# Mixture-of-experts stage of a two-block kernel: transposes moved into the products, full-height index matmuls, contiguous weight units

## The chip, the cores and the metric

The kernel runs on one core of a Trainium2 chip. Time is the device time of one execution in microseconds (us), as the median of several runs; lower is better. The profile is one further execution, recorded by the hardware profiler.

## The reference

The reference is two transformer-like blocks over 1024 tokens of 1024 channels, all in float32. The first block has a modulated RMS norm, an mLSTM and a Fourier branch, and then a mixture of experts in which each of 16 experts chooses its 128 tokens. The second block is a mixer of five branches with an output projection. The change touches the expert stage most, which is this:

```python
def expert_choice(h, w_router, w_gate, w_up, w_down):
    cap = CAP_FACTOR * l // N_EXPERTS                     # 128 tokens for each expert
    aff = jax.nn.softmax(jnp.einsum('bld,de->ble', h, w_router).astype(jnp.float32), axis=-1)
    vals, idx = lax.top_k(jnp.swapaxes(aff, 1, 2), cap)
    xs = h[bidx, idx]
    hid = jax.nn.silu(jnp.einsum('becd,edf->becf', xs, w_gate)) * jnp.einsum('becd,edf->becf', xs, w_up)
    y = jnp.einsum('becf,efd->becd', hid, w_down) * vals[..., None].astype(h.dtype)
    return jnp.zeros_like(h).at[bidx, idx].add(y)
```

Each of the three matrices of an expert is 1024 x 1024 float32, 4 MB.

## The kernel before

**Exact products.** Every float32 operand of a large product is split into a float32r part `hi` and a remainder `lo`; `mm3` (line 354) adds three matmuls, hi*hi, hi*lo and lo*hi. A matmul here has 128 rows, 128 stationary columns and 512 moving columns.

**Weights.** All weights pass through one list of units of 1 MB, 8 KB for each of the 128 partitions, made in `add_px` (line 577). `_issue` loads the next unit on SyncE's (SP's) DMA queue, in the order of the list, into a slot named `raw`. `_split` (line 234) makes slots named `w` from it: ScalarE writes `hi`, VectorE writes `lo`. A unit of an expert matrix holds two blocks of 128 rows and gives two `w` slots, each good for six matmuls. There are 25 slots of 8 KB a partition in all; `prefetch` (line 263) keeps up to 6 split `w` slots live, 5 ahead of the product, and gives the slots that are left to raw units. `pick` takes the free slot whose last user is due to finish first. An expert matrix unit is read by `k2` (line 605) as two pieces of 4 KB for each partition, 512 KB apart in DRAM.

**Experts.** `experts` (line 1629) works on one expert after the other. `index(e)` (line 1657) finds the tokens of expert e: two matmuls whose operands have 48 rows, each followed by a VectorE count over 512 columns, and a small add. `gather(e)` fetches the 128 token rows by an indirect DMA on GpSimd's (POOL's) queue into `xs`. `transp` (line 1676) turns a 128 x 1024 tile with eight TensorE transposes in two groups of four; after each group ScalarE writes 512 columns of `hi` and VectorE 512 columns of `lo` of a slot named `xT`. `prod` (line 1690) is one product: eight steps k of six matmuls, 48 in all, into two PSUM banks. For expert e the order on TensorE is

1. `prod(xT[e])` with the up matrix; VectorE then multiplies it into `g[e]`,
2. `transp(xs[e + 1])` (line 1739), then up to two calls of `index` (line 1742),
3. `prod(xT[e + 1])` with the gate matrix of the next expert, and ScalarE's silu,
4. `transp(g[e])` (line 1747) gives `hT`,
5. `prod(hT)` with the down matrix (line 1754), scaled by VectorE, and added to the tokens in DRAM by an indirect accumulating DMA on POOL's queue (the scatter, `x1d<-xs,idx` in the profile).

The index calls exist for the experts 0 to 6 only; there are 16 indices and the first three are made ahead of the loop. The last expert's rows are added on chip in `second`, the start of the second block.

Each instruction goes through `Queue.call` (line 67), so every row of the profile bears line 67, and tiles tell the rows apart: `pm` are the PSUM banks of products, `pa` those of transposes, indices and small things; `pa<-kc,xs` is a transpose of `transp`, `pa<-cm,one` an index matmul.

Of the kernel before, what the change touches and what calls it, by code (L numbers as in the profile page):

```python
# [29 lines left out]
# columns of the host-laid-out vector tile  # L30
C_C, C_CC, C_G1, C_G2, C_GF, C_BA = 0, 8, 16, 24, 32, 40
C_WC = 56                 # 9 taps x 8 blocks
C_CA = C_WC + 72          # 3 taps x 2
C_DW = C_CA + 6           # 31 taps x 2
# [5 lines left out]
# constant table columns  # L40
# [13 lines left out]
class Queue:  # L54
    """an engine of the core that books what is given to it in the plan"""
# [15 lines left out]
class Plan:  # L71
    """the core with its engines, and about when each of them gets to what it has been given, in microseconds:
    background work is given to an engine when its operands are about to be there"""
# [79 lines left out]
class Kern:  # L153
# [27 lines left out]
    # ---- memory  # L181
    def slot(self, dt=FT, name="t"):
        """8 KB a partition"""
        s = Slot()
        assert self.free_slots, "out of slots: " + " ".join(sorted(x.c for x in self.live.values()))
        s.i, s.c = self.free_slots.pop(self.pick()), name
        self.live[s.i] = s
        self.n += 1
        s.t = self.sp.tile([128, SLOT], dt, tag=f"s{s.i}", name=f"{name}_{self.n}")
        self.tags[s.i] = s.t.tensor.tag  # L190
        return s

    def pick(self):
        """the slot that is done with first"""
# [19 lines left out]
    # ---- weights: raw units of 8 KB a partition, split into two hi/lo pairs  # L214
# [75 lines left out]
    def get_raw(self):  # L290
        """next unit that is used as it comes"""
# [12 lines left out]
    # ---- background work  # L304
# [3 lines left out]
    def pump(self, us=1.3):  # L308
        """lets background work of about us microseconds be issued in each lane"""
# [9 lines left out]
    def until(self, *aps):  # L319
        """waits in the background until the tensor engine would not wait for these"""  # L320
# [3 lines left out]
    def soon(self, *aps):  # L324
        """near the end of the routing: the vector engine sorts until these are there"""
# [5 lines left out]
    def calm(self, eng="DVE", lead=None):  # L331
        """waits in the background until the engine has not much to do"""
# [20 lines left out]
    # ---- arithmetic helpers  # L353
    def mm3(self, ps, w, h, start, stop):
        """ps += w^T h for pairs (hi, lo) of exact splits"""
# [5 lines left out]
    def inv_sqrt(self, out, v, scale, eps):  # L361
        """out = 1 / sqrt(v * scale + eps)"""
# [8 lines left out]
    def bcast(self, src, n):  # L371
        """[128, n] read of n contiguous DRAM floats, the same for all partitions"""
        return bass.AP(tensor=src.tensor, offset=src.offset, ap=[[0, 128], [1, n]])

    # =====================================================================
# [6 lines left out]
    def consts(self):  # L382
# [36 lines left out]
        self.slotc = self.kc[:, K_SL:K_SL + 1]  # L419
        nc.vector.tensor_copy(self.one[0:32], self.idn[0:32, 0:16])  # L420
# [10 lines left out]
    # ---------------------------------------------------------------------  # L431
    def start(self):
# [50 lines left out]
        # shift and scale of x and of the context: silu(c) @ w_ada[:, :2048], channels on partitions  # L483
# [93 lines left out]
    def add_px(self):  # L577
# [7 lines left out]
        for i in range(2):  # L585
            self.add(self.I["w_f"][i], "g")
        wa = self.I["w_ada"]
        ada = (wa[k * 256:(k + 1) * 256, 2048 + ch * 1024:3072 + ch * 1024].rearrange("(k p) m -> p k m", p=128)
               for ch in range(4) for k in range(4))
# [15 lines left out]
        k2 = lambda m, i: m[i * 256:(i + 1) * 256].rearrange("(k p) m -> p k m", p=128)  # L605
        for i in range(4):
            self.add(k2(self.I["w_out"], i), "k")
# [11 lines left out]
        for m, e in order:  # L619
            for i in range(4):  # L620
                self.add(k2(m[e], i), "k")
# [5 lines left out]
        for i in self.order2[::2]:  # L627
            self.add(k2(self.I["w_out_2"], i // 2), "k")

    # ---------------------------------------------------------------------  # L630
    def chan(self, w, hs, evac, cols=128, order=None):
        """one block of output channels on partitions; hs: per 512 tokens the (hi, lo) of each k"""
# [21 lines left out]
    def tok(self, wa, wb, h, t, evac):  # L654
        """token tile t of a 256-column unit; wa, wb: k 0..3 and 4..7"""
# [11 lines left out]
    # ---------------------------------------------------------------------  # L667
    def load_wg(self):
# [6 lines left out]
        # kinds: input gate, forget gate of the two directions  # L675
# [7 lines left out]
    def gates(self, ps, T, m0, gcol, kinds, after):  # L683
        """ps: banks of raw gates [100, T]; leaves per-token columns in gcol and calls after(views)"""
# [36 lines left out]
        # chunk-local inclusive sums of the log forget gates, running from either end  # L721
# [38 lines left out]
    # ---------------------------------------------------------------------  # L760
    def conv(self, raw, out, blk, rows, tail):
        """depthwise 3x3 (SAME) of one channel block over a grid of rows x L/rows"""
# [28 lines left out]
    # ---------------------------------------------------------------------  # L791
    def ctx_pass(self):
# [12 lines left out]
        def after(v):  # L805
            # the states that the context leaves
# [62 lines left out]
    # ---------------------------------------------------------------------  # L869
    def px_front(self):  # L870
# [14 lines left out]
        # q, k  # L885
# [34 lines left out]
    # ---------------------------------------------------------------------  # L920
    def fourier_in(self):
# [38 lines left out]
        def fold(tmp, src, sgn, i, P, dst, n):  # L960
            """src [P, 4 x 128] in PSUM: channels c and 128 - c of each group together, then hi/lo"""
# [43 lines left out]
    def fourier(self):  # L1005
# [6 lines left out]
        # spectrum over the tokens k = 0..512: P even, Q odd  # L1012
        P, Q, Px = self.slot(FR, "P"), None, self.slot(FR, "Px")

        def pq(s, t, x):
            """hi, lo of chunk x of tile t"""
# [31 lines left out]
        # channel transform folded into w_fourier, then the product, half of the output channels at a time  # L1048
# [58 lines left out]
    # ---------------------------------------------------------------------  # L1107
# [24 lines left out]
    def ada_step(self, n):  # L1132
        """one unit of the other modulation vectors: products summed over the partitions at the end"""
# [1177 lines left out]
```

## Time and profile before

| | |
|---|---|
| time, median of 3 runs | 2015.81 us (2014.33 to 2016.72) |
| span of the profiled execution (first to last instruction) | 2013.5 us |
| TensorE busy | 1901.8 us, 94% |
| VectorE busy | 1430.7 us, 71% |
| ScalarE busy | 893.2 us, 44% |
| GpSimd busy | 207.4 us, 10% |
| moved by DMA | 361.03 MB, mean 179 GB/s |

The profiled execution has no time of its own beside its span; the span is 2.3 us under the median of the timed runs. The busy shares are means over stages with different limits. The expert stage lies from about 870 us to about 1505 us of the span. The granted clock of TensorE is given as a share of 2.4 GHz: 1.00 is 2.4 GHz, 0.50 is 1.2 GHz, and a value between them is a mean over both.

### The profile page before, as it was taken

To read this page: it belongs to the slowest core of one execution; us is meant where nothing else is said; L and a number is where in the kernel's file an instruction comes from. 1 tells how busy PE (TensorE), PEld (TensorE's weight loads), DVE (VectorE), ACT (ScalarE), POOL (GpSimd) and SP (SyncE) were. 2 spreads that over 40 slices of the span, in tenths; PEclk is the share of its full clock that TensorE was granted. 3 is DMA by queue.
4 is the path that set the end of the run, shared out by engine and by line. 5 is a ranking of instruction groups with operands and counts; after the bars stand their busy time and mean duration, and the time that the engine had idled before them with its cause. 6 is when DMAs were issued, how large, how long until landed. Compare 5 with 4: busy or idle time off the path is not lost.

```text
span 2013.5 us, 23979 instructions
## 1 busy us (share of the span) xinstructions
PE 1901.8 (94%) x9258; PEld 1523.0 (76%) x9258; DVE 1430.7 (71%) x2110; ACT 893.2 (44%) x1256; POOL 207.4 (10%) x186
## 2 busy tenths in 40 slices
PE   7899999999999999769999999999998999999997
PEld 3687888888877777557777777777777987678786
DVE  7797775556644547779889988888884787663544
ACT  5623432222322242346677677777765223433300
POOL 1300000000000034531001001101010000000011
PEclk9899999999999999879999999999999999999999
DMA  8101126434234343668989999999961101011322
GB/s 344 63 26 33 32 105 231 157 126 147 74 126 141 121 155 128 251 255 314 338 316 358 341 386 367 359 361 370 364 244 45 53 21 42 27 43 42 107 82 74
DMA packets 92317, 361.03 MB, mean 179 GB/s; under 512 B 9742, under 2 KB 10775, under 8 KB 85932
## 3 DMA queue, kind: packets, MB, share of 16 engines
q1 hardware_dynamic: 78156, 318.17, 42.0%
q0 software_dynamic: 9952, 35.42, 5.8%
q10 hardware_dynamic: 4096, 5.91, 0.9%
q8 instruction: 73, 1.20, 0.3%
q14 instruction: 40, 0.33, 0.0%
HBM read 329.96 MB, written 29.52 MB: 179 GB/s over the span
## 4 chain that ended last, share of the span: by engine, by line
PE 82%; DVE 10%; ACT 4%; issue 2%; DMA 2%; POOL 0%; ACTq 0%; POOLq 0%; DVEq 0%; SPq 0%
PE pm L67 73%; PE pa L67 9%; DVE w L67 2%; DVE tk L67 2%; ACT w L67 1%; DVE xs L67 1%; DMA bd<-gd 1%; DVE gt L67 1%; DVE mw L67 1%; DVE xT L67 1%; DVE tx L67 1%; ACT xT L67 0%; DMA wgr<-in_w_g 0%; DVE tm L67 0%; ACT gt L67 0%
## 5 line engine op out<-in xcount | busy, mean ns | idle before, releaser
L67 DVE TENSOR_TENSOR w<-raw,w 128x1024 fp32r<-128x1024 f32 (+1 forms) x496 | 590.6, 1226 | 104.7 <-ACT w L67 94.4
L67 ACT ACTIVATE w<-raw 128x1024 fp32r<-128x1024 f32 (+1 forms) x504 | 515.8, 1055 | 143.1 <-PE pm L67 125.1
L67 PE MATMUL pm<-w,xT 128*128 128x512 f32 x2304 | 556.0, 400 | 19.8 <-DVE xT L67 8.4
L67 PEld LDWEIGHTS pm<-w,xT 128*128 128x128 f32 x2304 | 434.2, 190 | 135.6 <-DVE xT L67 19.2
L67 PE MATMUL pm<-hT,w 128*128 128x512 f32 x1536 | 382.6, 400 | 0.0
L67 PEld LDWEIGHTS pm<-hT,w 128*128 128x128 f32 x1536 | 283.6, 190 | 60.4 <-issue 1.7
L67 PE MATMUL pm<-x,w 128*128 128x512 f32 x1152 | 281.0, 399 | 0.0
L67 PEld LDWEIGHTS pm<-x,w 128*128 128x128 f32 x1152 | 213.9, 188 | 53.8 <-issue 8.4
L67 PE MATMUL pm<-w,hh 128*128 128x512 f32 x480 | 111.3, 393 | 0.9 <-DVE w L67 0.9
L67 PEld LDWEIGHTS pm<-w,hh 128*128 128x128 f32 x480 | 90.2, 188 | 21.9 <-DVE w L67 1.3
L67 PE MATMUL pm<-w,mg 128*128 128x512 f32 x384 | 97.3, 402 | 0.0
L67 PEld LDWEIGHTS pm<-w,mg 128*128 128x128 f32 x384 | 69.5, 188 | 16.1 <-issue 1.5
L67 POOL DMA_INDIRECT x1d<-xs,idx x16 | 36.4, 2273 | 426.1 <-DVE xs L67 374.3
L67 DVE SCALAR_TENSOR_TENSOR qk<-raw,cols,qk 128x945 f32<-128x945 f32 (+2 forms) x64 | 78.0, 1219 | 1.3
L67 DVE SCALAR_TENSOR_TENSOR dg<-da,cols,dg 128x1023 f32<-128x1023 f32 (+29 forms) x60 | 76.0, 1267 | 1.6
L67 DVE TENSOR_TENSOR xT<-pa,xT 128x512 fp32r<-128x512 f32 x64 | 41.2, 684 | 25.5 <-ACT xT L67 25.5
L67 ACT ACTIVATE b<-pm 128x512 f32<-128x512 f32 x32 | 19.1, 598 | 66.4 <-PE pm L67 63.5
L67 POOL TENSOR_SCALAR sm<-sm 128x1 f32<-128x1 f32 x16 | 11.2, 702 | 362.5 <-DVE sm L67 361.7
L67 PE MATMUL pm<-om,w 128*128 128x512 f32 x192 | 46.6, 404 | 1.7 <-ACT om L67 0.9
L67 PEld LDWEIGHTS pm<-w,hT 128*128 128x128 f32 x384 | 46.0, 189 | 2.2 <-ACT w L67 0.9
L67 PE MATMUL pm<-w,hT 128*128 128x256 f32 x384 | 46.8, 283 | 0.2 <-DVE w L67 0.2
L67 PEld LDWEIGHTS pm<-w,x 128*128 128x128 f32 x384 | 45.7, 189 | 0.1
(364 smaller groups left out, 2070.8 us busy)
## 6 DMA issues: line engine op xcount, KB each, us to landing
raw<-in_w_gate SPq DMA_DIRECT2D x64, 1024.0 KB, 9.1
raw<-in_w_down SPq DMA_DIRECT2D x64, 1024.0 KB, 6.0
raw<-in_w_up SPq DMA_DIRECT2D x63, 1024.0 KB, 12.8
raw<-in_w_in SPq DMA_DIRECT2D x34, 1024.0 KB, 5.7
raw<-in_w_ada SPq DMA_DIRECT2D x24, 1024.0 KB, 7.8
raw<-in_w_out SPq DMA_DIRECT2D x9, 1024.0 KB, 4.9
b<-yd SPq DMA_DIRECT2D x16, 512.0 KB, 3.6
h2d<-tx POOLq DMA_DIRECT2D x8, 520.0 KB, 3.1
```

The source lines that it names most:

```text
L67: return f(*a, **kw)
```

## The change

It has four parts. (a) `transp` does one group of four transposes; `prod` takes a function that it calls after each step k; the transposes of `xs[e + 1]` are issued inside the up product of expert e after the steps k = 2 and k = 4, and those of `g[e]` inside the gate product of expert e + 1 after the same steps. The slot for the result is taken at k = 2. The last expert's `g` is turned between the products, as before. (b) The two `index` calls of an iteration are issued inside the down product, after k = 2 and k = 5. (c) The index matmuls read all 128 rows: `cm` is zeroed first on GpSimd, and the constant `one` on VectorE. (d) The host lays out the expert matrices, `w_out`, `w_out_2` and the later columns of `w_ada` such that a unit is one 8 KB piece for each partition and 1 MB in a row in DRAM; the first 2048 columns of `w_ada` become an array of their own. The rest of the diff takes comments out.

```diff
         self.slotc = self.kc[:, K_SL:K_SL + 1]
+        nc.vector.memset(self.one.bitcast(FT), 0.0)
         nc.vector.tensor_copy(self.one[0:32], self.idn[0:32, 0:16])
...
-        wa = self.I["w_ada"]
-        ada = (wa[k * 256:(k + 1) * 256, 2048 + ch * 1024:3072 + ch * 1024].rearrange("(k p) m -> p k m", p=128)
-               for ch in range(4) for k in range(4))
+        ada = (self.I["w_ada_rest"][ch * 4 + k] for ch in range(4) for k in range(4))
...
-        k2 = lambda m, i: m[i * 256:(i + 1) * 256].rearrange("(k p) m -> p k m", p=128)
         for i in range(4):
-            self.add(k2(self.I["w_out"], i), "k")
+            self.add(self.I["w_out"][i], "k")
...
             for i in range(4):
-                self.add(k2(m[e], i), "k")
+                self.add(m[e * 4 + i], "k")
...
         cs, cm = self.slot(FT, "cs"), self.slot(FR, "cm")
+
+        nc.gpsimd.memset(cm.t[:, 0:1024].bitcast(FT), 0.0)
...
-                nc.tensor.matmul(ps, self.one[0:48, e:e + 1].to_broadcast([48, 128]), cum[:, n * 512:(n + 1) * 512],
+                nc.tensor.matmul(ps, self.one[:, e:e + 1].to_broadcast([128, 128]), cm.t[:, n * 512:(n + 1) * 512],
                                  start=True, stop=True)
...
-        def transp(src):
-            o = self.slot(FR, "xT")
+        def transp(src, o, k4):
+
             hi, lo = (o.t[:, i * 1024:(i + 1) * 1024] for i in range(2))
-            for k4 in range(2):
-                p = self.bank("pa", (4, 128))
-                for k in range(4):
-                    kk = k4 * 4 + k
-                    nc.tensor.transpose(p[:, k], src[:, kk * 128:(kk + 1) * 128], self.idn)
...
-        def prod(o):
+        def prod(o, between=None):
+
             pss = [self.bank("pm") for _ in range(2)]
...
                 self.done(w)
+                if between:
+                    between(k)
             return pss
+
+        def turned(src, dst, key):
+
+            def between(k):
+                if k == 2:
+                    dst[key] = self.slot(FR, "xT")
+                if k in (2, 4):
+                    transp(src, dst[key], k // 2 - 1)
+            return between
...
-            pu = prod(xT[e])
+            pu = prod(xT[e], turned(xs[e + 1].t, xT, e + 1) if e + 1 < NE else None)
             self.free(xT.pop(e))
...
             if e + 1 < NE:
-                xT[e + 1] = transp(xs[e + 1].t)
                 if e + 2 < NE:
                     gather(e + 2)
-                for i in range(2 * e + 3, min(2 * e + 5, NE)):
-                    index(i)
-                if 2 * e + 4 == NE:
-                    self.free(cm)
-                g[e + 1] = silu(e + 1, prod(xT[e + 1]))
-            hT = transp(g.pop(e))
+                g[e + 1] = silu(e + 1, prod(xT[e + 1], turned(g[e], hT, e)))
             if e == NE - 1:
-                # the last rows are added to the tokens on chip, too: one-hot rows of their places
+                hT[e] = self.slot(FR, "xT")
+                for k4 in range(2):
+                    transp(g[e], hT[e], k4)
+
...
-            pd = prod(hT)
-            self.free(hT)
+            def next_indices(k):
+                i = 2 * e + 3 + (k - 2) // 3
+                if k in (2, 5) and i < NE:
+                    index(i)
+            pd = prod(hT[e], next_indices)
+            self.free(hT.pop(e))
+            if 2 * e + 4 == NE:
+                self.free(cm)
...
-    A["w_ada"] = f(g["w_ada"][0])
+
+    pairs = lambda w: f(w.reshape(-1, 2, 128, 1024).transpose(0, 2, 1, 3))
+    A["w_ada"] = f(g["w_ada"][0][:, :2048])
+    A["w_ada_rest"] = pairs(g["w_ada"][0][:, 2048:].reshape(1024, 4, 1024).transpose(1, 0, 2))
...
-    A["w_gate"], A["w_up"], A["w_down"] = (f(g[n][0]) for n in ("w_gate_e", "w_up_e", "w_down_e"))
+    A["w_gate"], A["w_up"], A["w_down"] = (pairs(g[n][0]) for n in ("w_gate_e", "w_up_e", "w_down_e"))
```

## Rows read from the trace of the kernel before

**Rows 1.** Head of the page.

```profile
span 2013.5 us, 23979 instructions
```

**Rows 2.** Timeline of TensorE (start, us, engine, line, operation), one late expert.

```profile
1203.44 1.03 PE L67 MATMUL pa<-kc,xs 128*128 128x128 f32 x8
1204.77 22.67 PE L67 MATMUL pm<-w,xT 128*128 128x512 f32 x96 [0.30 <-ACT xT L67]
1227.28 1.04 PE L67 MATMUL pa<-kc,xs 128*128 128x128 f32 x8
1228.57 0.73 PE L67 MATMUL pm<-w,xT 128*128 128x512 f32 x2 [0.25 <-ACT xT L67]
1230.28 10.86 PE L67 MATMUL pm<-w,xT 128*128 128x512 f32 x46 [0.98 <-DVE xT L67]
1240.98 1.03 PE L67 MATMUL pa<-kc,xs 128*128 128x128 f32 x8
```

**Rows 3.** Timeline of TensorE, between two products of an early expert.

```profile
1032.93 0.72 PE L67 MATMUL pa<-cm,one 48*128 48x512 f32 x2
1034.94 1.09 PE L67 MATMUL pa<-cm,one 48*128 48x512 f32 x2 [1.30 <-DVE xT L67]
1035.96 12.98 PE L67 MATMUL pm<-w,xT 128*128 128x512 f32 x48
```

**Rows 4.** Windows (busy by engine, clock, DMA share, GB/s): that product.

```profile
1036.00:1049.00 13.00, 13.00 (x52) 10.42 (x52) 11.37 (x18) 6.65 (x8) 0.00 (x0) 0.87 1.00 374
```

**Rows 5.** Timeline of TensorE, behind the up products 0, 7, 14, 15.

```profile
911.83 1.03 PE L67 MATMUL pa<-kc,xs 128*128 128x128 f32 x8
...
1189.75 1.04 PE L67 MATMUL pa<-kc,xs 128*128 128x128 f32 x8
...
1452.21 1.03 PE L67 MATMUL pa<-kc,xs 128*128 128x128 f32 x8
...
1490.08 1.33 PE L67 MATMUL pa<-kc,xs 128*128 128x128 f32 x8
```

**Rows 6.** Windows: the late experts, one of them, and the start of the second block.

```profile
1166.16:1466.13 299.97, 287.77 (x1283) 228.76 (x1282) 267.22 (x257) 223.64 (x241) 29.44 (x15) 1.00 0.98 368
1203.66:1241.21 37.55, 36.01 (x163) 28.59 (x162) 33.41 (x32) 27.96 (x31) 3.88 (x2) 1.00 0.98 364
...
1525.00:1550.00 25.00, 25.00 (x126) 20.38 (x125) 11.51 (x17) 14.24 (x21) 1.21 (x2) 1.00 0.00 1
```

**Rows 7.** Waits (engine, tile <- waited for: us, times, longest), 1166 to 1466 us.

```profile
ACT w L67 <- PE pm L67: 54.5, 120, 1.7
...
ACT w L67 <- DMA raw<-in_w_down: 5.0, 3, 1.7
```

**Rows 8.** Timeline of TensorE, start of the second block.

```profile
1540.29 1.63 PE L67 MATMUL pm<-x,w 128*128 128x512 f32 x6
1541.76 0.60 PE L67 MATMUL pa<-kc,x 128*128 128x128 f32 x4
1542.11 0.93 PE L67 MATMUL pm<-x,w 128*128 128x512 f32 x3
```

**Rows 9.** Groups of VectorE by form, 880 to 1000 us: the counts of an index.

```profile
L67 DVE TENSOR_SCALAR_CACHE_REDUCE ga<-pa,kc 128x512 f32<-128x512 f32 x14 | 9.9, 743 | 0.0
```

**Rows 10.** Timeline of GpSimd, first gather.

```profile
873.08 1.05 POOL L67 DMA_INDIRECT xs<-h2d,idx  x1 [15.09 <-issue]
```

**Rows 11.** Windows: DMA in one late expert, and at the start.

```profile
1244.60:1246.70 2.10, 2.10 (x11) 1.73 (x10) 2.10 (x3) 2.03 (x3) 0.00 (x0) 1.00 0.31 72
1256.00:1265.00 9.00, 9.00 (x42) 7.31 (x41) 7.65 (x7) 6.76 (x7) 1.43 (x1) 1.00 1.03 319
...
5.00:15.00 10.00, 2.87 (x7) 0.78 (x8) 5.97 (x10) 4.49 (x9) 0.00 (x0) 1.00 1.02 420
25.00:35.00 10.00, 10.00 (x45) 3.57 (x43) 7.39 (x9) 8.91 (x14) 0.90 (x2) 1.00 1.03 410
```

**Rows 12.** Waits of SP's DMA queue, 1166 to 1466 us.

```profile
SPq L67 <- DMA x1d<-xs,idx: 26.4, 8, 4.3
```

More of the change, by code (lines that the diff above doesn't have):

```diff
@@ L627, in add_px @@
         for i in self.order2[::2]:
-            self.add(k2(self.I["w_out_2"], i // 2), "k")
+            self.add(self.I["w_out_2"][i // 2], "k")
     def chan(self, w, hs, evac, cols=128, order=None):
@@ L1674, in gather @@
             xs[e] = s
-        def transp(src):
-            o = self.slot(FR, "xT")
+        def transp(src, o, k4):
             hi, lo = (o.t[:, i * 1024:(i + 1) * 1024] for i in range(2))
-            for k4 in range(2):
-                p = self.bank("pa", (4, 128))
-                for k in range(4):
-                    kk = k4 * 4 + k
-                    nc.tensor.transpose(p[:, k], src[:, kk * 128:(kk + 1) * 128], self.idn)
-                pf = p.rearrange("p a b -> p (a b)")
-                c = slice(k4 * 512, (k4 + 1) * 512)
-                nc.scalar.activation(hi[:, c], pf, AF.Copy)
-                nc.vector.tensor_sub(lo[:, c], pf, hi[:, c].bitcast(FT))
-            return o
-        def prod(o):
+            p = self.bank("pa", (4, 128))
+            for k in range(4):
+                kk = k4 * 4 + k
+                nc.tensor.transpose(p[:, k], src[:, kk * 128:(kk + 1) * 128], self.idn)
+            pf = p.rearrange("p a b -> p (a b)")
+            c = slice(k4 * 512, (k4 + 1) * 512)
+            nc.scalar.activation(hi[:, c], pf, AF.Copy)
+            nc.vector.tensor_sub(lo[:, c], pf, hi[:, c].bitcast(FT))
+        def prod(o, between=None):
             pss = [self.bank("pm") for _ in range(2)]
@@ L1719, in experts @@
             self.done(w)
-        xT = {0: transp(xs[0].t)}
+        xT, hT = {0: self.slot(FR, "xT")}, {}
+        for k4 in range(2):
+            transp(xs[0].t, xT[0], k4)
         index(2)
@@ L1738, in experts @@
             if e + 1 < NE:
-                xT[e + 1] = transp(xs[e + 1].t)
                 if e + 2 < NE:
                     gather(e + 2)
-                for i in range(2 * e + 3, min(2 * e + 5, NE)):
-                    index(i)
-                if 2 * e + 4 == NE:
-                    self.free(cm)
-                g[e + 1] = silu(e + 1, prod(xT[e + 1]))
-            hT = transp(g.pop(e))
+                g[e + 1] = silu(e + 1, prod(xT[e + 1], turned(g[e], hT, e)))
             if e == NE - 1:
+                hT[e] = self.slot(FR, "xT")
+                for k4 in range(2):
+                    transp(g[e], hT[e], k4)
                 x2 = [self.slot(FT, "x2") for _ in range(4)]
@@ L2219, in layout @@
     A["ctx"] = f(g["ctx"][0])
-    A["w_ada"] = f(g["w_ada"][0])
+    pairs = lambda w: f(w.reshape(-1, 2, 128, 1024).transpose(0, 2, 1, 3))
+    A["w_ada"] = f(g["w_ada"][0][:, :2048])
+    A["w_ada_rest"] = pairs(g["w_ada"][0][:, 2048:].reshape(1024, 4, 1024).transpose(1, 0, 2))
     bb = g["b_ada"][0]
     A["b_rows"] = f(np.concatenate([bb[2048:].reshape(4, 1024), g["g_norm2"][0][None]]))
-    A["w_out"] = f(g["w_out"][0])
+    A["w_out"] = pairs(g["w_out"][0])
     A["w_r"] = f(g["w_router"][0].reshape(8, 128, 16).transpose(1, 0, 2))
-    A["w_gate"], A["w_up"], A["w_down"] = (f(g[n][0]) for n in ("w_gate_e", "w_up_e", "w_down_e"))
+    A["w_gate"], A["w_up"], A["w_down"] = (pairs(g[n][0]) for n in ("w_gate_e", "w_up_e", "w_down_e"))
     A["w_in_2"] = f(g["w_in_2"][0].reshape(8, 128, 14, 256).transpose(2, 1, 0, 3))
@@ L2228, in layout @@
     A["memT"] = f(g["mem_2"][0].T.reshape(8, 128, 256).transpose(1, 0, 2))
-    A["w_out_2"] = f(g["w_out_2"][0])
+    A["w_out_2"] = pairs(g["w_out_2"][0])
     A["cc_pw"] = f(g["cc_pw_w_2"][0])
```

## The prediction, made before the changed kernel was run

> **What bounds the kernel now.** I read the page's head for the span [rows 1], then the windows: the change touches the expert stage, some 600 of 2013.5 us. There three resources are nearly full at once: in one late expert of 37.55 us TensorE (PE) is busy 36.0, VectorE 33.4, and the DMA engines show a share of 0.98 [rows 6]. The waits tell which one leads. ScalarE, which begins every weight split, waits 54.5 us for PE to release a slot and 5.0 us for a load [rows 7]: weights are ready and back up behind PE, so PE sets the pace. PE's timeline then shows what it does beside products [rows 2]. From the transposes at 1203.44 to those at 1240.98 an expert takes 37.54 us. The reader should see the holes: 1204.77 - 1203.44 = 1.33 us for eight transposes and the wait for their copy, 1.29 us for the next eight, and then two matmuls that are followed by 0.98 us of idling for VectorE's half of `xT`. The products run without a hole: 96 matmuls in 22.51 us, 46 in 10.70, two in about 0.47, together 33.68, so 0.234 us a matmul. 37.54 - 33.68 = 3.86 us an expert are not product.
>
> Early experts are slower. Between two of their products PE also does index matmuls and idles 1.30 us for VectorE [rows 3], and the product that follows takes 12.98 us, where 48 x 0.234 = 11.2. Its window says why: a granted clock of 0.87 over 13 us, which is 3.4 us at the lower level of 1.2 GHz, or 1.7 us lost [rows 4]. Between the ends of the up products 0 and 7 lie 277.92 us, 39.7 an expert; between 7 and 14, 262.46 us, 37.5 an expert; up product 15 ends 37.87 us later [rows 5].
>
> **The change part by part.** *Transposes inside products.* Same instructions, same count; what goes is the wait for the copies, because `xT` and `hT` are wanted only by the next product. What stays is PE's own time for four groups of four an expert. The start of the second block has such groups in a running product: six matmuls and a group take 1542.11 - 1540.29 = 1.82 us, less 6 x 0.234 = 0.42 for the group [rows 8]. Bounds: 0.35, its start to the next matmul's, and 0.60, its own length. I take 0.42, the same situation. So a late expert costs 33.68 + 4 x 0.42 = 35.36 us, 2.18 less (35.1 to 36.1).
>
> Do the copies come in time? The hidden work is ScalarE's and VectorE's part of `xT`, in their queues between splits. Splits run five units ahead of PE, a unit being 6 x 0.234 = 1.40 us, so 7 us of split weights stand between these copies and a PE stall. For `hT` the multiply by the up product must be done before k = 2 of the gate product ends, 18 x 0.234 = 4.2 us after the up product; it is two VectorE instructions. The rows of `xs[e + 1]` are gathered an iteration before. The slot of `xT` is held for most of a product longer, so raw units have one slot fewer.
>
> *Index matmuls.* Four an expert for experts 0 to 5 and two for 6, 26 in all, at 0.234 inside a product (up to 0.36, half of the row's 0.72 for two [rows 3]): 6.1 us. Full rows cost nothing by themselves, the columns being the same. In their old place they cost the 1.30 us of idling, their own time and, in four of the seven, the dip of the clock. With neither idling nor short work between products I expect no dip.
>
> *VectorE.* It becomes tight early: 33.4 us an expert [rows 6] plus four counts of 743 ns [rows 9], 36.4, beside PE's 35.36 + 4 x 0.234 = 36.30. I charge 0.2 us for each of six experts, 1.2, and about 2 us for the first up product, where splits are hardly ahead yet: 3 in all.
>
> *Zeroing.* The fill of `cm` goes to GpSimd, which idles 15.09 us before the first gather [rows 10], so less than that is hidden; that of `one` is at the very start of the kernel. Nothing.
>
> *8 KB pieces.* At the start of the kernel, 8 KB pieces (`w_ada`) come at 420 GB/s, 4 KB pieces (tokens) at 410 [rows 11]. The bounds are thus nothing and 2.4% of load time. Nothing waits for loads here, so I book nothing. But loads must keep up: 364 GB/s x 37.55 us = 13.64 MB an expert. For 9 us of it a scatter runs beside the loads, and all together move 319 GB/s, 2.9 MB [rows 11]; the other 10.8 MB at 410 to 420 take 26 us: 35 us, under the 35.36 that PE will want, with nothing to spare. Today's slack is the 2.1 us around 1245 with 72 GB/s [rows 11]. Outside the expert stage I book nothing: its 8 KB loads were hidden behind products with slots to wait for.
>
> *Sum.* Up 0 to up 7: 7 x 35.36 + 6.1 = 253.6 against 277.9, saves 24.3. Up 7 to up 14: 247.5 against 262.5, saves 14.9. Up 14 to up 15, with only two groups: 33.68 + 0.84 = 34.5 against 37.9, saves 3.4. Up 0 gets two groups, 0.8 more. 24.3 + 14.9 + 3.4 - 0.8 = 41.8, less 3 for VectorE and the start: 38.8. The span goes from 2013.5 to 1975 us; the median of the runs lies 2.3 us above the span, so 1977 us.
>
> A rule of the Trainium skill speaks against the change, on the page TensorE: Matmul & The Clock Gate, section Part 4: PE-mode transpose: transposes don't count as work for the clock as matmuls do. It is weighed as the last rival; the trace does not bear it out for groups of four, with its 1.00 in the second block.
>
> **The rivals.**
> 1. *VectorE becomes the bound.* Its queue is in order, and each turned tile can make it wait for PE's transposes. If it loses 0.98 us [rows 2] at each of two tiles, 33.4 + 2.0 = 35.4 changes nothing late, but early it is 38.4: 6 x 38.4 + 37 = 267, which saves 11 instead of 24. With the late 14.9 and 2.6 of the ends: 2015.8 - 28 = 1988. For it: busy 0.89 of the time already. Against: 7 us of lead.
> 2. *Loads become the bound.* If the 2.1 us of slack are only SP waiting for slots and stay, a late expert keeps its 37.5 us and an early one falls to that: 277.9 - 7 x 37.5 = 15.4, so 2000 us. For it: share 0.98. Against: ScalarE hardly waits for loads now.
> 3. *Slower: the scatter starves beside larger pieces.* SP already waits 26.4 us in eight experts for a scatter to land, because a raw unit takes its slot [rows 12]. If loads of 8 KB take twice the turns' length against the scatter's 4 KB rows, its 9 us become 18. Half of the added 9 us is covered by loads still queued, 4.5 are lost: 35.1 + 4.5 = 39.6 us an expert, 2.1 more than now in 15, +31, less the 15 of rival 2: 2032 us. It decides once more than 3.4 us an expert are lost (2.4 of slack, 1 for the early gain). Against: weight loads have slots ready well ahead. On the page DMA: Bandwidth & Descriptors, sections Queues, rings and completion order and SWDGE vs HWDGE vs iDMA, the Trainium skill says that a DMA engine turns from one queue to the next only between packets, and that packets are best kept to 4096 bytes. No run here has yet shown 8 KB pieces beside a scatter.
> 4. *The change doesn't do what it says:* PE's wait returns at another place of the product, or the dips stay with index matmuls. Four dips alone are 6.8 us, which leaves 1984, within the forecast's range; only all of it together gives no change, 2015.
> 5. *Slower: the clock falls inside products.* With a dip of 1.7 us at each of four groups an expert would take 35.4 + 6.8 = 42.2, 4.7 more than a late one: 15 x 4.7 = 70, less 15: 2070. Against: in the second block the clock stays at 1.00 from 1525 to 1550 with groups of four between matmuls [rows 6, 8].
>
> **How the numbers follow.** Forecast (PE bound, 1977): 0.57. VectorE (1988): 0.17. Loads (2000): 0.12. No change: 0.05. Scatter (2032): 0.07. Clock (2070): 0.02. The low end is the forecast without its 3 us of losses and with groups at 0.35, 15 x 4 x 0.07 = 4 us: 1970, and a us for faster loads, 1969. At 0.60 a group costs 11 us more, 1988. The high end takes in the loads' case, 2001; outside remain the slower ones and no change. Measured against no change, 0.2% or 4 us is about what a timing of this kernel can tell. Faster: 0.57 + 0.17 + 0.12 = 0.86; same 0.05; slower 0.09.
>
> **What would show it.** In PE's timeline the matmuls of a late expert should run without an idle entry, three products in about 35.4 us, with groups of four in between that cost 0.42; the clock should be 1.00 in every window from 930 us on, index matmuls inside the down products; ScalarE should still wait for PE and not for loads. VectorE waits for `pa` with PE idle behind them would speak for rival 1; ScalarE waiting for `raw` loads, with a DMA share above 1.0 throughout, for rival 2; a scatter that lands much later and longer waits of SP for it, for rival 3; a clock under 1.00 behind the groups, for rival 5. The prediction is wrong above all if a second resource turns out to need the time that PE frees: all three stand within 2% of each other.

## The result, and the profile after

The changed kernel takes 1969.91 us (median of 4 runs, 1967.04 to 1971.36) where the kernel before takes 2016.26 us beside it (4 runs): a ratio of 0.9771, with a 95% interval of 0.9760 to 0.9783. The forecast was 1977 us with a range of 1969 to 2001, so the time lies in the range, at its low end: 46 us were saved where 39 were forecast. One execution of each of two experiments, of 10533 and 6539 us, lay far above all others and is left out of every median and ratio below. The profiled run took 1969.11 us; its page begins with the span, and its DMA part says how many packets the same 361 MB travelled in (92317 before, 64541 now):

```profile
span 1967.3 us, 23992 instructions
...
DMA packets 64541, 361.03 MB, mean 184 GB/s; under 512 B 9742, under 2 KB 10775, under 8 KB 30380
```

The chain of work that ended last in the changed kernel, through one late expert (start, us, what; `pa` x4 is a group of four transposes, `pm` are product matmuls). It answers to [rows 2]:

```profile
1190.88 0.44 PE pa L67 x4
1191.32 2.79 PE pm L67 x12
1194.11 0.44 PE pa L67 x4
1194.54 8.34 PE pm L67 x36
1202.88 0.44 PE pa L67 x4
1203.32 2.76 PE pm L67 x12
1206.08 0.44 PE pa L67 x4
1206.52 19.39 PE pm L67 x84
1225.91 0.44 PE pa L67 x4
```

There is nothing in it but TensorE (PE): no wait, no idle entry, and from 930 to 1400 us neither PE nor its weight loads wait for anything. An expert takes 1225.91 - 1190.88 = 35.03 us where it took 37.54. Four groups are 4 x 0.44 = 1.76 us, and the 144 matmuls of three products the other 33.27, so 0.231 us a matmul. In an early expert two index calls stand in the down product, as the same chain shows further up:

```profile
928.62 0.46 PE pa L67 x2
929.08 4.10 PE pm L67 x18
933.19 0.46 PE pa L67 x2
933.65 6.93 PE pm L67 x30
```

They cost 0.92 us an expert and nothing around them. Windows of the changed kernel (busy us of PE, PE's weight loads, VectorE, ScalarE, GpSimd; clock; DMA share; GB/s): an early stretch, the late experts, one late expert, and 5 us in it during which a scatter runs beside the loads. They answer to [rows 4, 6, 11]:

```profile
1000.00:1025.00 25.00, 25.00 (x116) 20.39 (x116) 24.79 (x33) 17.56 (x19) 3.51 (x2) 1.00 1.00 365
1123.00:1423.00 300.00, 300.00 (x1375) 245.54 (x1374) 282.90 (x282) 234.86 (x261) 29.64 (x16) 1.00 1.01 393
1190.88:1225.91 35.03, 35.03 (x163) 28.62 (x161) 32.81 (x33) 27.25 (x30) 3.56 (x3) 1.00 1.02 406
1195.00:1200.00 5.00, 5.00 (x24) 4.06 (x23) 4.82 (x6) 4.60 (x6) 1.04 (x1) 1.00 1.04 320
```

PE is busy for all of it, and the granted clock is 1.00, early and late. VectorE has 0.21 us of 25 left in the early stretch and still PE does not wait for it. Waits of the changed kernel from 880 to 1460 us (engine, tile <- waited for: us, times, longest), ScalarE and PE first, SP's DMA queue behind; they answer to [rows 7, 12]:

```profile
ACT w L67 <- PE pm L67: 95.7, 173, 2.3
...
PE pm L67 <- POOL w L67: 3.4, 4, 1.9
...
ACT w L67 <- DMA raw<-in_w_gate: 1.6, 2, 0.8
```

```profile
SPq L67 <- DMA x1d<-xs,idx: 43.7, 2, 26.7
```

ScalarE backs up behind PE and not behind loads. PE's only waits for split weights are in the first gate product. SP's two waits for a scatter begin only at 1420 us, behind the loads of the experts; the one of 26.7 us ends with the read of the tokens for the second block, and the kernel before has one of 24.1 us there, too. In the experts SP no longer waits for a scatter. By stretches, with the ends of the up products of before from [rows 5], and those of after taken as the first `hT` group less 18 matmuls (at 916.68, 1167.76 and 1412.59 us in the chain) and, for the last, from the transposes at 1442.66 (the less sure forecast of the start adds the 2 us charged for the first up product):

| stretch | before | forecast | after | saved |
|---|---|---|---|---|
| end of up 0 to end of up 7 | 277.92 | 253.6 | 251.08 | 26.84 |
| up 7 to up 14 | 262.46 | 247.5 | 244.83 | 17.63 |
| up 14 to up 15 | 37.87 | 34.5 | 34.23 | 3.64 |
| start to up 0 | 911.83 | 912.6, less sure 914.6 | 912.52 | -0.69 |
| behind up 15 | 523.42 | 523.4 | 524.64 | -1.22 |

The saved times add up to 46.2 us, the difference of the spans. Two things were thus asked of the chip: which part of the change does this, and which of the three nearly full resources would stop it next.

### The profile page after: what moved, and what is told of

Its sections match the earlier page's. It is cut to its first block, busy times and chain, and to the rows that moved or that the text cites. A ratio compares the mean times of both kernels' runs of the same rounds, so it can differ in the third digit from the quotient of the medians.

```text
span 1967.3 us, 23992 instructions
## 1 busy us (share of the span) xinstructions
PE 1877.2 (95%) x9258; PEld 1516.7 (77%) x9258; DVE 1422.5 (72%) x2111; ACT 884.8 (45%) x1256; POOL 216.5 (11%) x187
## 2 busy tenths in 40 slices
DMA packets 64541, 361.03 MB, mean 184 GB/s; under 512 B 9742, under 2 KB 10775, under 8 KB 30380
## 3 DMA queue, kind: packets, MB, share of 16 engines
q10 hardware_dynamic: 4096, 5.91, 0.9%
## 4 chain that ended last, share of the span: by engine, by line
PE 87%; DVE 7%; ACT 2%; DMA 2%; issue 1%; POOL 1%; POOLq 0%; ACTq 0%; DVEq 0%; SPq 0%
PE pm L67 76%; PE pa L67 11%; DVE tk L67 2%; DMA bd<-gd 1%; DVE gt L67 1%; DVE tx L67 1%; POOL w L67 1%; DVE w L67 0%; DMA wgr<-in_w_g 0%; DVE tm L67 0%; ACT gt L67 0%; DMA b<-yd 0%; DVE mw L67 0%; ACT x L67 0%; ACT w L67 0%
## 5 line engine op out<-in xcount | busy, mean ns | idle before, releaser
L67 ACT ACTIVATE w<-raw 128x1024 fp32r<-128x1024 f32 (+1 forms) x504 | 510.3, 1052 | 106.1 <-PE pm L67 99.4
L67 PEld LDWEIGHTS pm<-w,xT 128*128 128x128 f32 x2304 | 429.4, 189 | 101.5 <-POOL w L67 5.6
L67 POOL DMA_INDIRECT x1d<-xs,idx x16 | 44.3, 2768 | 385.5 <-DVE xs L67 378.0
L67 ACT ACTIVATE xT<-pa 128x512 fp32r<-128x512 f32 x64 | 37.6, 590 | 30.1 <-PE pa L67 30.0
## 6 DMA issues: line engine op xcount, KB each, us to landing
raw<-in_w_up SPq DMA_DIRECT2D x63, 1024.0 KB, 12.4
```

Of the source, the lines that this page charges most:

```text
L67: return f(*a, **kw)
```

## The experiments

All times are medians; the kernel before ran beside each at 2015.5 to 2016.4 us. One profile varies by some 5 us ahead of the expert stage (index calls 0 and 1 begin between 865.3 and 870.4 us in kernels that are equal up to there), so parts of the change are compared within a profile: from the first transposes inside up product 0 to those of `hT` inside gate product 15, both read in the chain (with the idling put back, in the timeline). In the changed kernel this is 1412.59 - 904.66 = 507.93 us.

| kernel | time, us | this stretch, us |
|---|---|---|
| changed | 1969.9 | 507.93 |
| changed, 4 KB pieces | 1969.3 | 507.93 |
| changed, 48 rows | 1974.2 | 512.88 |
| changed, index calls between products | 1965.4 | 507.70 |
| transposes alone | 1972.5 | 510.43 |
| index calls between products, idling put back | 2009.7 | 551.41 |

**The layout, out and alone.** The changed kernel with the old arrays and units of two 4 KB pieces, and the kernel before with the new ones:

```diff
-                self.add(m[e * 4 + i], "k")
+                self.add(k2(m[e], i), "k")
...
-    A["w_gate"], A["w_up"], A["w_down"] = (pairs(g[n][0]) for n in ("w_gate_e", "w_up_e", "w_down_e"))
+    A["w_gate"], A["w_up"], A["w_down"] = (f(g[n][0]) for n in ("w_gate_e", "w_up_e", "w_down_e"))
```

> The changed kernel with the old layout: units again as two pieces of 4 KB a partition. Theory (TensorE sets the pace, loads keep up): the same as the changed kernel within 3 us, 1968 to 1973 us, products without idling, a late expert still 35.0 us. Rival (the larger pieces are what lets the loads keep up): loads of 4 KB need 35.1 us an expert by the rows of before, and with scatters in between up to 36; ScalarE then waits for raw loads and the time is 1975 to 1985 us.

> The kernel before with the new layout alone. Theory (nothing waits for loads in the kernel before): 2013 to 2016 us, no change that can be told. Rival (shorter load time is part of the gain): 2005 to 2010 us. In both the scatter's stretch of slow loads (9 us at 319 GB/s before) may become shorter, as it is about 5 us in the changed kernel.

Measured: 1969.32 us without it (ratio to before 0.9770, 0.9757 to 0.9782), and 2017.36 us with it alone (1.0007, 0.9998 to 1.0016). In the changed kernel with the old layout the stretch in the table is the same to 0.01 us, the packets are back at 92317, and ScalarE waits 3.2 us in all for loads, as with the new one. The layout is worth nothing here. That answers rival 3 as well: 4 KB and 8 KB pieces beside the scatters give one time, and from 1166 to 1400 us a scatter lands 11.8 us after its issue with 8 KB pieces and 10.5 us with 4 KB pieces (medians), far from twice as late. On the page DMA: Bandwidth & Descriptors, section SWDGE vs HWDGE vs iDMA, the Trainium skill says of the packets of a GpSimd queue that they are preferably of at most 4096 bytes; for the loads on SP's queue these two runs show neither gain nor loss from going beyond.

**48 rows again.** The changed kernel with index matmuls on 48 rows:

```diff
-                nc.tensor.matmul(ps, self.one[:, e:e + 1].to_broadcast([128, 128]), cm.t[:, n * 512:(n + 1) * 512],
+                nc.tensor.matmul(ps, self.one[0:48, e:e + 1].to_broadcast([48, 128]), cum[:, n * 512:(n + 1) * 512],
```

> The changed kernel with index matmuls of 48 rows again. Theory (the clock fell because TensorE idled and did short work between products, not because of the rows): the clock stays at 1.00 and the time is that of the changed kernel, 1968 to 1972 us. Rival (rows in use count for the clock): dips come back behind index matmuls, 1.7 us each, in at least four experts: 1977 us or more.

Measured: 1974.16 us, 0.9794 (0.9782 to 0.9807). Theory and rival were both wrong: the clock stays at 1.00, and still the stretch in the table is 4.95 us longer. The chain at the place shown above, and PE's waits from 900 to 1200 us, of this run:

```profile
928.50 0.65 PE pa L67 x2
929.15 4.33 PE pm L67 x18
933.48 0.65 PE pa L67 x2
934.13 7.08 PE pm L67 x30
```

```profile
PEld pa L67 <- issue: 4.7, 13, 0.4
PEld pm L67 <- issue: 4.3, 12, 0.4
```

Against the changed kernel a call costs 0.65 - 0.46 = 0.19 us more, and the matmuls behind it 0.23 or 0.15 more: 0.38 us for each trip from 128 rows to 48 and back, 13 times, 4.95 us. The waits say where: weight loads (PEld) stand for 0.4 us at each change of height, 13 times on the way in and 12 on the way out; with full rows neither line exists. Full rows don't "cost nothing by themselves", they gain. On the page TensorE: Matmul & The Clock Gate, section Step-by-step: what each phase is for, the Trainium skill says of the weight load that the number of rows does not matter to its time; by that alone the two kernels would be equal, and the trace does not agree where heights change.

**Index calls in their old place,** between the up and the gate product, full rows:

```diff
                     gather(e + 2)
+                for i in range(2 * e + 3, min(2 * e + 5, NE)):
+                    index(i)
...
-            pd = prod(hT[e], next_indices)
+            pd = prod(hT[e])
```

> The changed kernel with the index calls back between the up and the gate product, transposes still inside, full rows. Theory (what cost was TensorE's wait for the transposes' PSUM banks, 1.3 us, and the dip behind it): without transposes between the products nothing is waited for; no idling, no dip, 1969 to 1973 us. Rival (the place between products costs by itself): 1.3 us of idling in seven experts and four dips of 1.7 us, together 16 us: 1985 us.

Measured: 1965.42 us, 0.9748 (0.9736 to 0.9761), below the 1969 to 1973 that were expected and faster than the changed kernel if anything; the stretch is 0.2 us shorter, so most of the 4 us is not the expert stage's. In the chain four index matmuls stand between the products, and no wait:

```profile
943.01 4.14 PE pm L67 x18
947.15 0.92 PE pa L67 x4
948.07 4.20 PE pm L67 x18
```

Moving the calls is worth nothing once no transposed tile is waited for between the products.

**Full rows alone,** in the kernel before:

```diff
+        nc.gpsimd.memset(cm.t[:, 0:1024].bitcast(FT), 0.0)
...
-                nc.tensor.matmul(ps, self.one[0:48, e:e + 1].to_broadcast([48, 128]), cum[:, n * 512:(n + 1) * 512],
+                nc.tensor.matmul(ps, self.one[:, e:e + 1].to_broadcast([128, 128]), cm.t[:, n * 512:(n + 1) * 512],
```

> The kernel before with full-height index matmuls as its only change. Theory (the run with 48 rows in the changed kernel cost 4.8 us in 13 index calls): what full rows save is the cost of switching the row count, about 0.37 us a call, and here as there 13 calls lie on the path: 4 to 5 us less than before, 2011; the early products keep their granted clock of 0.87 behind the index matmuls. Rival 1: the 48 rows are what lets the clock fall behind index matmuls; full rows take the dips of 1.7 us away as well, four to seven of them: 2000 to 2005, and the early products show 1.00. Rival 2: in their old place the index matmuls stand beside an idle PE anyway, so their length is hidden: 2015.6, no change.

Measured: 2008.09 us, 0.9956 (0.9942 to 0.9969), with runs from 2005 to 2012, between the 2011 of the theory and the 2000 to 2005 of rival 1. The timeline of PE, two early experts:

```profile
990.48 1.10 PE L67 MATMUL pa<-cm,one 128*128 128x512 f32 x2 [1.50 <-DVE xT L67]
991.41 11.25 PE L67 MATMUL pm<-w,xT 128*128 128x512 f32 x48
...
1029.37 1.19 PE L67 MATMUL pa<-cm,one 128*128 128x512 f32 x2 [1.47 <-DVE xT L67]
1030.35 12.81 PE L67 MATMUL pm<-w,xT 128*128 128x512 f32 x48
```

The dip of the clock (12.8 us for 48 matmuls) is in three of the six early products with four index matmuls ahead, where it was in four of six: rival 1 is refuted, full rows don't hold the clock up, and idling of 1.5 us is still there. From up 0 to up 7 the stretch is 1185.19 - 910.02 = 275.17 us, 2.75 less than before, of which one dip fewer is 1.6. The other 5 us of the median are not in the expert stage of this profile (its span is only 3.6 us shorter than before), and what they are stays open.

**The transposes alone.** The kernel before with part (a) of the change and nothing else:

```diff
-            pu = prod(xT[e])
+            pu = prod(xT[e], turned(xs[e + 1].t, xT, e + 1) if e + 1 < NE else None)
...
-                g[e + 1] = silu(e + 1, prod(xT[e + 1]))
+                g[e + 1] = silu(e + 1, prod(xT[e + 1], turned(g[e], hT, e)))
```

> The kernel before with the transposes inside the products as its only change; index matmuls keep 48 rows and their place between the products, pieces stay at 4 KB. Theory: the transposes carry nearly the whole gain. The runs so far put the pieces at 0, the place of the index calls at 0 to 4 us in favour of the old place, the rows at 4.8: 1969.9 + 4.8 - 2 = 1973 us (1969 to 1976), with a granted clock of 1.00 throughout. Rival: without full rows or without the move the dip of the clock behind the index matmuls comes back, 1.7 us in at least four of seven early experts: 1978 to 1985, and early gate products at 0.87.

Measured: 1972.47 us, 0.9783 (0.9769 to 0.9796), clock 1.00 from 900 to 1460 us. The rows are dearer by a trip to 48 rows and back per pair of calls, as this chain shows beside the last one:

```profile
946.91 1.12 PE pa L67 x4
948.04 4.39 PE pm L67 x18
```

1.12 - 0.92 and 4.39 - 4.20 are 0.39 us, seven times 2.7, and the stretch is 510.43 - 507.70 = 2.73 us longer. So the transposes carry 44 of the 46 us, full rows 2.7 in the old place and 5 in the new one (both with the transposes inside), and the move and the layout nothing.

**Idling put back.** The run with the index calls between the products, and a product of two columns that waits for a count:

```diff
                     index(i)
+                    if i % 2:
+                        nc.tensor.matmul(self.bank("pa")[:, 0:2], self.idn, self.idf[:, 2:4], start=True, stop=True)
```

> The run with the index calls between the up and the gate product (full rows, 1965.4, no fall of the clock), and behind the first of the two calls a TensorE product of two columns that needs the call's count, so that TensorE idles there for 1 to 4 us in each of the early experts, as it did before the change; transposes stay inside the products. Theory: idling is what lowered the clock behind index matmuls; the early gate products show 0.87 or so again in at least half of the experts, so that the time rises by 7 idle times and four or more dips of 1.7 us: 7 x 2 + 7 = 21, 1986 (1978 to 1998). Rival: the clock fell because eight transposes, two index matmuls and an idle time came together; idling alone leaves the clock at 1.00 and costs just itself, 1979 at 7 x 2 us.

Measured: 2009.68 us, 0.9966 (0.9954 to 0.9978). PE's timeline at one of seven places, and windows early and late:

```profile
996.03 0.62 PE L67 MATMUL pa<-cm,one 128*128 128x512 f32 x2
1000.33 0.39 PE L67 MATMUL pa<-idf,kc 128*128 128x2 f32 x2 [3.67 <-DVE ga L67]
1000.57 1.20 PE L67 MATMUL pa<-cm,one 128*128 128x512 f32 x2
1001.57 5.45 PE L67 MATMUL pm<-w,xT 128*128 128x512 f32 x18
```

```profile
950.00:1150.00 200.00, 181.69 (x787) 146.54 (x786) 172.46 (x203) 130.81 (x145) 14.18 (x9) 0.95 0.88 324
1200.00:1400.00 200.00, 200.00 (x918) 163.84 (x917) 187.43 (x184) 156.79 (x173) 19.38 (x11) 1.00 1.01 390
```

The time lies above the expected range, because the idle time was longer than expected (3.1 to 3.7 us, 25 us in seven). The mechanism held: the clock is 0.95 over the early stretch and 1.00 late, and the 18 matmuls behind each of the seven idle times take 5.3 to 6.9 us from start to start, where they take 4.2 without: 12.8 us in seven. The stretch in the table is 43.7 us longer than in the run without the idling, 25.0 of it idle time, 12.8 in those matmuls, and the other 5.9 in the small matmuls between. Transposes stand inside the products here. So idling of this length lowers the clock without transposes beside it, and index matmuls without idling don't (the runs with the index calls between the products and with the transposes alone). For the shorter idling of the kernel before, 1.0 to 1.3 us, it is not shown that idling alone is enough: its late experts idle for up to 0.98 us at a time between matmuls of products [rows 2], and their clock is 1.00 [rows 6].

**More VectorE work:**

```diff
+        if mode == "k" and self.limit_kv + 2 <= u < self.limit2 - 2 and self.s_done % 8 == 0:
+            nc.vector.tensor_sub(lo, src, hi.bitcast(FT))
```

> The changed kernel; in every eighth weight split VectorE's part is done twice, three in an expert, 3 x 1.15 = 3.5 us of added VectorE work an expert, without effect on the values. Theory: VectorE has 0.4 us of slack in an early expert (busy 24.6 to 24.8 of 25 us in the windows) and 1.5 to 2 us in a late one, so it becomes the bound at once: 3 us more in each of 7 early experts, 1.5 to 2 more in each of 8 late ones, some 35 us: 2005 (1995 to 2012). Rival: busy spans of VectorE hold waiting for the port or for operands, and there is more room than they show: less than 10 us, 1980 at most.

Measured: 2001.43 us, 0.9926 (0.9911 to 0.9941), as the theory said. Windows early and late, and what PE now waits for from 950 to 1400 us (the row is of transposes into `hT`, which wait for VectorE's multiply by the up product):

```profile
950.00:1150.00 200.00, 187.59 (x837) 148.38 (x835) 199.14 (x231) 141.81 (x153) 19.52 (x11) 1.00 0.98 349
1150.00:1400.00 250.00, 244.50 (x1111) 197.98 (x1112) 249.24 (x249) 192.77 (x208) 39.87 (x14) 1.00 1.00 381
```

```profile
PE pa L67 <- DVE xs L67: 13.7, 12, 1.4
```

VectorE is full, and PE idles for 12.4 us in 200 early and 5.5 in 250 late. The mechanism of rival 1 is real. By the windows of the changed kernel VectorE has about 0.3 us an expert left early (0.21 of 25) and 2 us late (17.1 of 300).

**More loads:** 15 copies of 1 MB in SP's queue, from DRAM to DRAM.

```diff
+        if 12 <= i < 192 and i % 12 == 0:
+            r = slice((i // 12 - 1) * 256, (i // 12) * 256)
+            self.loader.dma_start(self.spill[r].rearrange("(k p) m -> p k m", p=128), self.units[u][0])
```

> The changed kernel with one more transfer of 1 MB in each of 15 experts on SyncE's queue, a copy of a weight unit from DRAM to a part of DRAM that nothing reads. Theory (the loads had nothing to spare in the prediction, and in the windows they move 406 GB/s of the 420 to 430 that a busy stretch reaches): some 2.5 us of transfer are added to each expert and at most 1 us is hidden, 15 x 1.5 to 2.5 us = 22 to 38: 1992 to 2008. ScalarE then waits for raw loads. Rival: the units that are loaded ahead and SyncE's waits for slots are real slack, and the copies are hidden: 1970 to 1975.

Measured: 1969.74 us, 0.9775 (0.9760 to 0.9790), no change: the theory fell. The page counts 376.76 MB, so the copies were made. Windows of this run (late experts, and the end of the loads), then the end of the loads in the changed kernel:

```profile
1123.00:1423.00 300.00, 300.00 (x1374) 245.61 (x1373) 283.88 (x282) 236.66 (x260) 29.66 (x16) 1.00 1.02 406
1420.00:1430.00 10.00, 10.00 (x45) 8.11 (x44) 9.96 (x10) 8.40 (x10) 0.00 (x0) 1.00 1.01 422
1430.00:1440.00 10.00, 10.00 (x45) 8.12 (x45) 9.69 (x10) 6.29 (x7) 9.19 (x1) 1.00 0.82 339
```

```profile
1420.00:1430.00 10.00, 10.00 (x45) 8.08 (x44) 9.85 (x9) 8.68 (x11) 0.00 (x0) 1.00 0.69 284
1430.00:1440.00 10.00, 10.00 (x45) 8.16 (x44) 10.00 (x11) 7.70 (x8) 7.15 (x1) 1.00 0.00 0
```

In the late stretch 406 GB/s are moved instead of 393, and the loads end some 11 us later; at an estimated 2.5 us a copy (1.05 MB at 420 GB/s), 37 us of transfers went mostly into gaps and for the rest into the lead that the loads have. A DMA share of 1.01 did not mean that the loads were at their limit: SP's queue waits for slots that PE and VectorE release, 240 and 208 us in the changed kernel from 880 to 1460 us. With the copies these waits are 188 and 156 us, and SP waits 101 us for earlier transfers instead: that is the room that the copies took. The lead is used up in part, so this shows 15 copies in 15 experts and not more.

**The first weight splits.** PE waits for split weights in the first gate product alone, 3.4 us for GpSimd, which splits the first four `w` slots, and 1.3 us for ScalarE. The first run leaves GpSimd one of the four:

```diff
-        (nc.gpsimd if u in self.pool_lo else nc.vector).tensor_sub(lo, src, hi.bitcast(FT))
+        pool = u in self.pool_lo and (u < self.limit_kv + 2 or (u, j) == (self.limit_kv + 2, 0))
+        (nc.gpsimd if pool else nc.vector).tensor_sub(lo, src, hi.bitcast(FT))
```

> The changed kernel; of the first four weight splits of the experts only the first is left on GpSimd, the other three go to VectorE. Theory: TensorE, which now sets the pace from the first product on, waits about 9 us there for GpSimd's slow splits (11.34 us for four), of which half is due anyway while the queue of splits fills: 4 to 5 us less, 1965. Rival: VectorE is as late as GpSimd there, or the lead of splits that is lost at the start comes back as a wait in the early experts, where VectorE is busy for over 0.96 of the time: 1970, no change.

On top of it, index call 2 inside the first gate product:

```diff
-        index(2)
...
-        g = {0: silu(0, prod(xT[0]))}
+        g = {0: silu(0, prod(xT[0], lambda k: index(2) if k == 5 else None))}
```

> As the run with the first splits on VectorE, and index call 2, which stands ahead of the first gate product, is issued inside that product. Theory: two index matmuls and their counts no longer stand ahead of the first weight splits on VectorE: 1 to 2 us less than the run with the first splits alone, 1964. Rival: the gather of the third expert's rows, which needs this index, comes later and its transposes in the up product of expert 1 wait for it, or nothing was waiting for the counts: the same as the run with the first splits alone.

And the first run again, with no split of the experts' weights left on GpSimd:

```diff
-        pool = u in self.pool_lo and (u < self.limit_kv + 2 or (u, j) == (self.limit_kv + 2, 0))
+        pool = u in self.pool_lo and u < self.limit_kv + 2
```

> The changed kernel with all first weight splits of the experts on VectorE, the very first one too. Theory: TensorE still waits 1.95 us for GpSimd's first split in the run with the other three on VectorE; a split takes VectorE 1.15 us in place of 2.8, so 1 to 1.6 us less than that run, 1961.5. Rival: VectorE is busy with the counts of index call 2 just then and begins the first split later than GpSimd does; no gain, or up to 1 us lost: 1963 to 1964.

Measured: 1962.94 us (0.9742, 0.9728 to 0.9755), 1966.44 (0.9749, 0.9736 to 0.9762) and 1964.21 (0.9746, 0.9732 to 0.9759). PE's timeline of the first gate product in the changed kernel, and then with three splits on VectorE:

```profile
884.65 1.84 PE L67 MATMUL pm<-w,xT 128*128 128x512 f32 x6 [1.95 <-POOL w L67]
887.01 2.93 PE L67 MATMUL pm<-w,xT 128*128 128x512 f32 x6 [0.52 <-POOL w L67]
890.32 2.78 PE L67 MATMUL pm<-w,xT 128*128 128x512 f32 x6 [0.39 <-POOL w L67]
893.64 11.02 PE L67 MATMUL pm<-w,xT 128*128 128x512 f32 x47 [0.54 <-POOL w L67]
```

```profile
878.90 16.80 PE L67 MATMUL pm<-w,xT 128*128 128x512 f32 x65 [1.94 <-POOL w L67]
```

From the first transposes of `xT` to those inside up product 0 it is 21.85 us instead of 25.07, a gain of 3.2. With index call 2 moved it is 22.37, with the last split on VectorE as well 21.98: those two add nothing, as their rivals said (in the last one PE waits 2.07 us for VectorE's first split where it waited 1.94 for GpSimd's), and three kernels of one stretch show how far medians scatter (1962.9 to 1966.4). The first of them is the fastest version run: it beats the changed kernel as well as the one before, by 3 us that the trace shows; its median says 7.

## Why the prediction was right

*Transposes inside products: right, and nearly all of the gain.* The copies come in time, the groups cost 0.44 us (0.42 taken), and PE is never idle. With this part alone 44 of 46 us are there.

*The mis-sized term: a matmul of a product.* The prediction took 33.68 us for 144 matmuls, 0.234 each, from runs said to be without a hole. The rows of PE hide holes: the timeline of the kernel before, at the start of that run, has weight loads that wait for the two copies of `xT` under matmul rows that are shown as one piece (start, us, ...; in brackets the wait):

```profile
1204.77 0.30 PEld L67 LDWEIGHTS pm<-w,xT 128*128 128x128 f32 x2 [0.54 <-ACT xT L67]
...
1205.50 2.16 PEld L67 LDWEIGHTS pm<-w,xT 128*128 128x128 f32 x10 [0.43 <-DVE xT L67]
```

So part of the wait that the change removes was counted as product time: the third load begins 0.73 us after the first, where two matmuls take 0.46, which is 0.27 of the 0.41 us (33.68 against 33.27) that three products were priced too high; where the other 0.14 lies is not shown. In the changed kernel a matmul takes 0.231 us, 0.003 less; over the 2160 matmuls of 45 products that is some 6.5 us, less 1.2 us for 58 groups that are 0.02 us dearer: about the 5.5 us by which the forecast of the three stretches (253.6 + 247.5 + 34.5 = 535.6) lies above the measured 530.1.

*Charged and not paid:* 3 us for VectorE and for the first up product. An early expert takes 251.08 / 7 = 35.87 us, which is 35.03 and its index matmuls and nothing else, with VectorE busy for 24.79 of 25; the first up product has no wait. VectorE's work came out lower than taken: the 33.4 us of a late expert are 32.81 in the changed kernel, and with four counts of 0.743 that is 35.8, under the 35.95 that PE takes with four index matmuls. The 1.2 us by which the rest of the kernel is longer were not in the sum.

*Full rows: wrong.* Booked at nothing, they are worth 5 us in the new place of the index calls. That the total has this gain all the same is luck: the sum took 0.234 us for an index matmul inside a product, the price of one with full rows; at 48 a matmul costs (2 x 0.65 + 0.23 + 0.15) / 4 = 0.42 us, outside the bound of 0.36.

*Index calls: right in size, wrong in part.* 26 matmuls cost 6.0 us and the dip is gone, but the move does neither: between the products they cost the same and the clock stays at 1.00. What takes the dip away is the move of the transposes, and the idling that went with it.

*8 KB pieces at nothing: right.* What was said of the loads, "nothing to spare", was wrong: 1 MB more an expert is hidden. (364 GB/s over 37.55 us are 13.67 MB and not 13.64, which changes nothing.) *Zeroing at nothing* is not contradicted: index calls 0 and 1 begin at 870.26 us, where they began at 869.82, within the 5 us by which profiles vary there.

*The rivals.* VectorE (1) did not bind, but is the next bound, 32 us for 3.5 us of work an expert. Loads (2) are refuted by the copies. The scatter (3): with one running all transfers together still move 320 GB/s, for some 5 us instead of 9, and with 4 KB pieces the time is the same; the longer wait of SP that was to be its sign (26.7 us) is there, but behind the experts' loads, and also with 4 KB pieces (26.8 us). No effect (4): the wait and the dips are gone and did not come back elsewhere. The clock inside products (5): 1.00 in all windows from 900 to 1450 us with four groups an expert. The rule of the Trainium skill that stood behind it (page TensorE: Matmul & The Clock Gate, Part 4: PE-mode transpose) made no difference to any time here: as groups of four between matmuls, transposes left the clock at its upper level, 2.4 GHz.

## What to carry to other kernels

Put short TensorE work whose result another engine must copy inside a long product, three to five steps of six matmuls ahead of its use: here the copies cost nothing there, and the idle time, behind which the clock fell, goes as well. Read a matmul's price from a stretch in which the weight loads don't wait either, for the wait that you mean to remove may already lie inside the runs that you price by. A resource whose busy share is near 1 need not be near its limit: ask it by an experiment with added work, as here, where VectorE bound at once and the DMA queues took 1 MB more in each of 15 experts without loss.

## What was not expected of the hardware

- Index matmuls of 48 rows among those of 128 cost 0.38 us for each trip to the other height and back, with weight loads that stand for 0.4 us at each change; of the same height they cost 0.23 us each, as a matmul of a product does.
- A DMA share of 1.01 to 1.02 stood at 393 GB/s and at 406 GB/s in the same stretch; the share did not tell how much more could be moved.
- Idling TensorE for 3.1 to 3.7 us between index matmuls lowered the clock behind it at all seven places, for 1.1 to 2.7 us lost a time; at 1.0 to 1.5 us it did so in seven of twelve places (the kernel before, and with full rows alone). With index matmuls and no idling it never fell, nor did it with up to 0.98 us of idling between matmuls of products (late experts of the kernel before).
